# A hymba streaming step on one core: a re-planned instruction order, with 45 weight remainders made by accumulating GpSimd transfers

## The chip, the cores and the metric

The kernel runs on one core of one Trainium2 chip. The metric is the device time of that core in microseconds (us), the median of three executions. One more execution was recorded by the hardware profiler, and all lines of a profile come from it. TensorE (PE in the profile) multiplies matrices; VectorE (DVE), ScalarE (ACT) and GpSimd (POOL) do elementwise work; SyncE (SP) issues the transfers between memory and SBUF. Each engine has its own queue of instructions and takes them in order; semaphores hold an instruction back until what it reads is there.

## The reference

One inference step of an encoder of two layers, on 512 frames of a new stream and 64 frames of a running one, which the kernel treats as one block of 576 columns. A layer is:

```python
proj = x @ w_in                       # 1024 x 2560: q, k, v, conv_a, conv_gate
q, k = rope(q, pos), rope(k, pos)     # 8 sub-heads of 64
a = softmax(q1 k1') - lam * softmax(q2 k2')   # 4 differential heads, masked by chunks
o = rmsnorm(a @ v) * sub_g * (1 - lam_init)
u = conv_a * sigmoid(conv_gate)
c = silu(layer_norm(causal_depthwise_conv(u, hist, conv_w, conv_b)))   # width 31
y = concat(o, c) @ w_out              # 1024 x 1024
x = layer_norm(ALPHA * x + y)
h = square(relu(x @ w_ff1))           # 1024 x 4096
x = layer_norm(ALPHA * x + h @ w_ff2)
```

Outputs are x of both streams, the new keys and values of both layers, and the last 30 columns of u. Everything is float32.

## The kernel before, in words

**Matrix products in three passes.** A float32 operand is split into a rounded part and a remainder. A weight `w` gives `wh` (ScalarE copies `raw` into a type that TensorE reads in one pass, L834) and `wl = raw - wh` (L837, a subtraction on VectorE or GpSimd). The product is `wh*xh + wh*xl + wl*xh`, three matmuls of 128x288 (L706, L707, L708). The columns go in two groups of 288.

**Weights.** The weights lie in DRAM as 92 units of 128x1024 for each layer: 20 for the input projection (conv gates and inputs 0 to 7, and q, k, v of four heads 8 to 19), 8 for the output projection (20 to 27) and 64 for the feed forward. `weights()` brings a unit: a transfer on SP's queue into one of two `raw` tiles, the copy on ScalarE, the subtraction. There are four pairs `wh`/`wl`; a unit makes 48 matmuls (8 blocks of rows, two column groups, three passes). The first two units come in four quarters each, so that TensorE can begin early. For layer 1 the 20 units of the input projection are split ahead of time, during the feed forward of layer 0, and stored to DRAM (`wscr`); they are loaded ready made. In the feed forward most products are Strassen-like, with sums of weight blocks formed on VectorE first (L2030) and split afterwards (L2003, L1831).

**Stages.** Each layer has a mixer (projection, attention heads, convolution, output projection), a layer norm, the feed forward and another layer norm. In the mixer the convolution takes 31 taps for each of four tiles: VectorE multiplies and adds most of them into a PSUM tile `sc` (L1284), ScalarE multiplies the rest into `prod` (L1269), and GpSimd adds those up in `r` (L1272). An attention block goes: scores on TensorE, the maximum on VectorE (L1433), the exponential on ScalarE (L1449), the difference of the two softmaxes on VectorE (L1477, tile `P`), transposes on TensorE (L1486), the product with v (L1515).

**What sets the order.** Nothing in the kernel is issued in the order in which the code stands. Every operation is a node with its engines and the cost on each, what it depends on, what buffers it takes and gives back, and a priority. `Sched.run` plays the whole program through with these costs (`cV`, `cA`, `cG`, `cD`, `cP`, and `delay` from engine to engine) and issues, at each planned moment, the ready node of highest priority; the instructions then stand in each engine's queue in that order. Where a node may run on two engines (a subtraction on VectorE or GpSimd) the plan chooses. VectorE and GpSimd share a port: a node marked `two`, and every node that may run on GpSimd, waits in the plan until the port is free. Planned times only decide the order; on the chip an instruction starts when its semaphores allow. `PHASES` holds eight sets of knobs (priorities, which squares go where, how many taps go to ScalarE and GpSimd) for the mixer, the output projection, the feed forward and its end, in each layer.

Of the kernel before, what the change touches and what calls it, by code (L numbers as in the profile page):

```python
# [135 lines left out]
PRP, PRS = 159.3, -11.0  # L136
# [133 lines left out]
 {'CS': 1,  # L270
  'CSTD': 2,
  'KA': 6,
  'KB': 8,
  'KR': 2,
# [11 lines left out]
  'PE_': 37.6,
  'PK': -502.6,
  'PN': 781.5,
  'PQ': 23.6,
  'PR': 47.2,  # L290
  'PS': 304.1,
  'PT': 1371.8,
# [2083 lines left out]
```

## Time and profile before

| | us |
|---|---|
| median of three executions | 1412.38 (1410.14 to 1413.55) |
| the profiled execution | 1412.93 |
| its span, first to last instruction | 1411.1 |
| TensorE busy | 1318.3 |
| VectorE busy | 1130.2 |
| ScalarE busy | 680.2 |
| GpSimd busy | 268.8 |

Mean granted clock of TensorE 0.969. A busy TensorE in this table is not a TensorE at full speed: matmuls overlap, a matmul counts as busy until its modelled end, and it takes longer under a lower granted clock. Where stages are compared, the number of matmuls begun in a stretch is the better measure. In a row of the stretches ("windows"), each engine has its busy time and in brackets how many instructions; then come the granted clock, the share of the DMA engines, and GB/s. In a list of waits the columns are the total, the number of waits and the longest. In a timeline they are the start, the duration, the engine, line, operation and tiles, and in square brackets the idle time before and what ended it.

### The profile page before, as it was taken

How to read it: one execution, taken by the hardware profiler on the slowest of the kernel's cores; microseconds unless marked ns; L12 is line 12 of the kernel's file. 1: busy time of each engine (PE TensorE's matmuls, PEld its weight loads, DVE VectorE, ACT ScalarE, POOL GpSimd, SP SyncE). 2: the span in 40 equal slices, each digit the busy share in tenths (PEclk: the TensorE clock that was granted, in tenths of full speed). 3: DMA queues.
4: the chain of work that ended last, by engine and by line, in shares of the span. 5: the costliest groups of instructions: out<-in, count | busy, mean ns of one | idle time of the engine just before them, and what ended most of it. 6: DMA issues, size and time to landing. Idle time of an engine off the chain costs nothing.

```text
span 1411.1 us, 24840 instructions
## 1 busy us (share of the span) xinstructions
PE 1318.3 (93%) x9512; PEld 1268.5 (90%) x9512; DVE 1130.2 (80%) x2251; ACT 680.2 (48%) x1388; POOL 268.8 (19%) x246
## 2 busy tenths in 40 slices
PE   6979699979899999999999989899899999999997
PEld 5979588979899999999988988689889999999996
DVE  6799998785888887978739899888768777777756
ACT  4656567254444445444246566642645343434414
POOL 0447510260000000000133684212400000000003
PEclk9999899999999999999999999799899999999998
DMA  6312134134265555555544432222122132313121
GB/s 200 97 61 80 41 105 144 60 98 134 93 196 170 195 162 179 180 179 182 181 151 166 148 127 100 81 86 62 44 83 98 61 120 75 105 61 116 58 68 68
DMA packets 63623, 162.79 MB, mean 115 GB/s; under 512 B 10128, under 2 KB 15888, under 8 KB 63504
## 3 DMA queue, kind: packets, MB, share of 16 engines
q1 hardware_dynamic: 63504, 161.20, 34.5%
q8 instruction: 75, 1.23, 0.4%
q14 instruction: 44, 0.36, 0.1%
HBM read 130.52 MB, written 30.65 MB: 114 GB/s over the span
## 4 chain that ended last, share of the span: by engine, by line
PE 70%; DVE 21%; ACT 4%; issue 2%; DMA 1%; POOL 1%; SPq 0%; ACTq 0%; DVEq 0%; POOLq 0%
PE b L706 21%; PE b L708 21%; PE b L707 21%; DVE sc L1284 7%; PE b L953 1%; DVE nm L1433 1%; DVE wl L837 1%; DVE P L1477 1%; PE b L1515 1%; PE sc L706 1%; PE sc L708 1%; POOL sq L1011 1%; PE sc L707 1%; DVE swp L1314 1%; DMA a<-in_xT_dram 1%
## 5 line engine op out<-in xcount | busy, mean ns | idle before, releaser
L706 PE MATMUL b<-x,wh 128*128 128x288 f32 x1364 | 418.4, 307 | 17.8 <-ACT wh L834 9.0
L708 PE MATMUL b<-x,wl 128*128 128x288 f32 x1364 | 406.9, 298 | 6.5 <-DVE wl L837 5.0
L707 PE MATMUL b<-x,wh 128*128 128x288 f32 x1364 | 406.9, 298 | 1.1 <-POOL x L1101 1.0
L706 PE MATMUL b<-a,wh 128*128 128x288 f32 x1088 | 326.9, 300 | 1.8 <-ACT P L1454 0.9
L707 PE MATMUL b<-a,wh 128*128 128x288 f32 x1088 | 323.1, 297 | 0.0
L708 PE MATMUL b<-a,wl 128*128 128x288 f32 x1088 | 322.4, 296 | 0.0
L706 PEld LDWEIGHTS b<-x,wh 128*128 128x128 f32 x1364 | 260.5, 191 | 27.5 <-ACT wh L834 10.3
L708 PEld LDWEIGHTS b<-x,wl 128*128 128x128 f32 x1364 | 260.1, 191 | 8.5 <-DVE wl L837 6.7
L707 PEld LDWEIGHTS b<-x,wh 128*128 128x128 f32 x1364 | 260.6, 191 | 3.0 <-POOL x L1101 1.8
L706 PEld LDWEIGHTS b<-a,wh 128*128 128x128 f32 x1088 | 206.6, 190 | 3.3 <-ACT P L1454 1.1
L707 PEld LDWEIGHTS b<-a,wh 128*128 128x128 f32 x1088 | 207.0, 190 | 0.5
L708 PEld LDWEIGHTS b<-a,wl 128*128 128x128 f32 x1088 | 206.6, 190 | 0.0
L1011 POOL TENSOR_TENSOR sq<-sq,sq 128x288 f32<-128x288 f32 x41 | 35.2, 883 | 765.5 <-ACT sq L1005 764.9
L834 ACT CAST wh<-raw 128x1024 fp32r<-128x1024 f32 (+1 forms) x118 | 118.7, 1006 | 125.0 <-PE b L707 89.7
L837 DVE TENSOR_TENSOR wl<-raw,wh 128x1024 fp32r<-128x1024 f32 (+1 forms) x113 | 135.4, 1201 | 28.8 <-ACT wh L834 28.4
L2220 DVE TENSOR_TENSOR r<-r,b 128x288 f32<-128x288 f32 x192 | 86.4, 451 | 76.3 <-PE b L708 76.2
L1272 POOL TENSOR_TENSOR r<-r,prod 128x606 f32<-128x606 f32 x75 | 115.9, 1545 | 116.7 <-ACT prod L1269 98.8
L1284 DVE SCALAR_TENSOR_TENSOR sc<-ub,par,sc 128x606 f32<-128x606 f32 x157 | 133.5, 851 | 3.7
L2003 ACT CAST wh<-ckv 128x512 fp32r<-128x512 f32 x104 | 64.0, 620 | 97.8 <-PE b L707 75.1
L1831 DVE TENSOR_TENSOR wl<-ckv,wh 128x512 fp32r<-128x512 f32 x104 | 71.1, 685 | 3.0 <-ACT wh L2003 2.9
L1269 ACT ACTIVATE prod<-ub,par 128x606 f32<-128x606 f32 x75 | 59.3, 802 | 23.2 <-POOL r L1272 22.9
L2003 ACT CAST wh<-ah 128x512 fp32r<-128x512 f32 x52 | 32.2, 620 | 53.3 <-PE b L707 52.2
(321 smaller groups left out, 2286.3 us busy)
## 6 DMA issues: line engine op xcount, KB each, us to landing
raw<-in_wu_dram SPq DMA_DIRECT2D x110, 512.0 KB, 3.7
wscr<-cs SPq DMA_DIRECT2D x80, 256.0 KB, 2.5
ckv<-in_wu_dram SPq DMA_DIRECT2D x26, 512.0 KB, 3.7
ah<-in_wu_dram SPq DMA_DIRECT2D x26, 512.0 KB, 4.4
cs<-in_wu_dram SPq DMA_DIRECT2D x40, 256.0 KB, 2.8
wh<-wscr SPq DMA_DIRECT2D x20, 512.0 KB, 3.3
wl<-wscr SPq DMA_DIRECT2D x20, 512.0 KB, 4.3
ckv<-in_ck_dram SPq DMA_DIRECT2D x8, 512.0 KB, 5.0
```

The lines of the kernel that those rows point to most:

```text
L706: TE.matmul(o, wh, xh, start=start, stop=False)
L707: TE.matmul(o, wh, xl, start=False, stop=False)
L708: TE.matmul(o, wl, xh, start=False, stop=stop)
L834: S.copy(wt["hi"][:, c], wt["raw"][:, c])
L837: e.tensor_tensor(wt["lo"][:, c], wt["raw"][:, c], wt["hi"][:, c].bitcast(F32), op=ALU.subtract)
L1011: e.tensor_tensor(q[a]["t"], q[a]["t"], q[b]["t"], op=ALU.add)
L1269: S.activation(st[j], ub[t][:, j:j + UC], AF.Copy, scale=w)
L1272: GP.tensor_tensor(cc[t], cc[t], st[j], op=ALU.add)
L1284: V.scalar_tensor_tensor(st["a0"], win(j), w, st["a0"], op0=ALU.mult, op1=ALU.add)
L1831: e.tensor_tensor(o, a, b, op=ALU.subtract)
L2003: S.copy(tl["wh"][box["i"]][:, off:off + n], src())
L2220: V.tensor_tensor(rr, rr, bk(), op=ALU.add)
```

## The change

The plan is made with other costs and knobs, and some weight remainders are made by transfers.

1. **45 units by accumulating transfers.** A new knob `DM` says which share of the units of a phase goes this way: 0.67 in the mixer and the output projection of layer 0, 0 in its feed forward, and 1 for the output projection, 0.5 for the feed forward and 1 for its last four units in layer 1. Such a unit is loaded into `raw` as before; ScalarE writes `wl = -raw` (L875 of the changed kernel), GpSimd's queue issues a transfer that reads the same unit from DRAM again and adds it into `wl` (L878), and ScalarE copies `raw` to `wh` (L881). No subtraction is left on VectorE or GpSimd for that unit, and `raw` is given back after the copy to `wh`. So `wl` becomes the difference between the weight and its rounded value. 16 of the 45 are in layer 0 (10 in the input projection, 6 in the output projection), 29 in layer 1 (8 in the output projection, 21 in the feed forward).
2. **The plan's model.** A transfer that only waits for the transfer before it on the queue no longer waits in the plan for that one's landing (`late`). Costs of ScalarE reading a PSUM bank, with one and with two per-partition operands, are told apart; delays between engines are a little smaller; what TensorE waits for gets 0.1 more. In the rule of the port only who is marked changes: the first step of the reciprocal root is marked, and the accumulating transfer is exempt.
3. **The knobs** of all eight phases.

The core of the diff:

```diff
-def cA(n, ptr=False):
-    return (0.19 if ptr else 0.09) + 0.00084 * n
+def cA(n, ptr=0, bank=False):
+    return (0.09 + 0.095 * ptr if not bank else 0.05) + 0.00084 * n
...
-PRP, PRS = 159.3, -11.0
+PD = 0.1
+DM, GD, GDL = 0.0, 0.88, 6.5
+PRP, PRS = 889.2, -10.4
...
-PHASES = [{'CS': 0,
+PHASES = [{'CH': 4,
+  'CS': 0,
   'CSTD': 2,
-  'KA': 2,
+  'DM': 0.67,
+  'KA': 4,
...
     def delay(a, b):
         if a == b:
-            return 0.0 if a in "PDN" else 0.12
+            return {"A": 0.08, "V": 0.03, "G": 0.05}.get(a, 0.0)
         if "N" in (a, b):
             return 0.0
-        return 0.25 if "P" in (a, b) else 0.15
+        return 0.2 if "P" in (a, b) else 0.13
...
+                            late = 0.0 if e == "D" and "D" in s.eng else n.lat
                             for o in s.eng:
-                                s.ready = max(s.ready, t + c + n.lat + min(self.delay(e, o) for o in s.eng))
+                                s.ready = max(s.ready, t + c + late + min(self.delay(e, o) for o in s.eng) + (PD if "P" in s.eng and e in "VAG" else 0.0))
...
+        chain["dm"] += 0.0 if start else DM
+        by_dma = not start and chain["dm"] >= 0.999
+        chain["dm"] -= by_dma
...
+            if by_dma:
+                def neg(e):
+                    slots()
+                    S.activation(wt["lo"], wt["raw"], AF.Copy, scale=-1.0)
+                def acc(e):
+                    GP.dma_start(wt["lo"], wu[l, i], accum_op=ALU.add)
+                def hi(e):
+                    S.copy(wt["hi"], wt["raw"])
+                wt["hin"] = m = op({"A": cA(D)}, neg, (chain["ld"], chain["hi"]), acq=("w",), pri=pri)
+                los.append(op({"G": GD}, acc, (m,), lat=GDL, pri=pri + 1000, two=False))
+                chain["hi"] = h = op({"A": cA(D)}, hi, (m,), rel=end, pri=pri)
+                his.append(h)
+                return
...
-        m = op({"V": 0.27}, start, (dep,), rel=rel, pri=pri)
+        m = op({"V": 0.27}, start, (dep,), rel=rel, pri=pri, two=True)
```

What the change makes of the instructions in all: TensorE's work is the same but for three small matmuls; VectorE's subtractions of 128x1024 for weights go from 105 to 65 and GpSimd's from 5 to none; ScalarE has 45 instructions more, the negations. Three places in the order follow; in them a line number is that of the kernel the rows come from, and the number behind a name tells buffers apart.

**The start, on SP's queue.** `a` are the tiles of x as they come in (eight tiles for each of the two column groups), `raw_81` and `raw_82` the two weight tiles; 128x256 is a quarter of a unit. Before, from the last tile of x on:

```order
L1149 DMA a_209<-in_xT_dram 128x288
L828 DMA raw_81<-in_wu_dram 128x256
L1181 DMA cs_259<-in_cst_dram 128x1152
L699 DMA par_161<-in_par_dram 128x169
L828 DMA raw_82<-in_wu_dram 128x256
L1382 DMA ckv_112<-in_ck_dram 128x1024
L745 DMA sgm_100<-in_par_dram 128x256
L699 DMA ident<-in_cst_dram 128x128
L828 DMA raw_82<-in_wu_dram 128x256
L699 DMA par_165<-in_par_dram 128x169
L745 DMA sgm_101<-in_par_dram 128x256
L828 DMA raw_82<-in_wu_dram 128x256 x2
```

Now, from the fourth quarter of the first unit on:

```order
L861 DMA raw_81<-in_wu_dram 128x256
L861 DMA raw_82<-in_wu_dram 128x256 x3
L1202 DMA a_230<-in_xT_dram 128x288
L861 DMA raw_82<-in_wu_dram 128x256
L1202 DMA a_240<-in_xT_dram 128x288
L1202 DMA a_187<-in_xT_dram 128x288
L861 DMA raw_81<-in_wu_dram 128x1024
L1202 DMA a_190<-in_xT_dram 128x288
L1202 DMA a_193<-in_xT_dram 128x288
L861 DMA raw_82<-in_wu_dram 128x1024
L1202 DMA a_195<-in_xT_dram 128x288
L1202 DMA a_201<-in_xT_dram 128x288
```

The second unit's quarters, the third and the fourth unit moved ahead of most of the second column group of x, and ahead of the tables (`cs`), the parameters and the cache (`ckv`), which come behind x now.

**The convolution of layer 0, on VectorE's queue.** The rows are in the second tile's taps (`ub_795`/`ub_801` is its input, `sc_119` the sum); `P` is the softmax difference of an attention block. Before:

```order
L1284 SCALAR_TENSOR_TENSOR sc_119<-ub_795,par_161,sc_119 128x2x303
L837 TENSOR_TENSOR wl_88<-raw_82,wh_84 128x1024
L1284 SCALAR_TENSOR_TENSOR sc_119<-ub_795,par_161,sc_119 128x2x303
L1477 SCALAR_TENSOR_TENSOR P_914<-P_914,rc_564 64x576
L1284 SCALAR_TENSOR_TENSOR sc_119<-ub_795,par_161,sc_119 128x2x303
L837 TENSOR_TENSOR wl_89<-raw_81,wh_85 128x1024
L1284 SCALAR_TENSOR_TENSOR sc_119<-ub_795,par_161,sc_119 128x2x303
L1322 TENSOR_TENSOR r_94<-r_94,swp_972 128x576
L1284 SCALAR_TENSOR_TENSOR sc_119<-ub_795,par_161,sc_119 128x2x303
L837 TENSOR_TENSOR wl_90<-raw_82,wh_86 128x1024
```

Now, around the same block of the same head:

```order
L1337 SCALAR_TENSOR_TENSOR sc_119<-ub_801,par_161,sc_119 128x2x303 x2
L1530 SCALAR_TENSOR_TENSOR P_921<-P_921,rc_599 64x576
L1337 SCALAR_TENSOR_TENSOR sc_119<-ub_801,par_161,sc_119 128x2x303 x5
L894 TENSOR_TENSOR wl_89<-raw_81,wh_85 128x1024
L1337 SCALAR_TENSOR_TENSOR sc_119<-ub_801,par_161,sc_119 128x2x303
```

Two of the three subtractions left this stretch; the `P` row stands 10 rows earlier in the queue than it did.

**The same stage on GpSimd's queue**, where `r` collects the taps that ScalarE multiplied. Before:

```order
L1272 TENSOR_TENSOR r_91<-r_91,prod_730 128x606
L1239 MEMSET ub_795 128x30
L837 TENSOR_TENSOR wl_87<-raw_81,wh_83 128x1024
L1272 TENSOR_TENSOR r_93<-r_93,prod_871 128x606
L1272 TENSOR_TENSOR r_93<-r_93,prod_886 128x606
```

Now:

```order
L878 DMA wl_88<-in_wu_dram 128x1024
L878 DMA wl_89<-in_wu_dram 128x1024
L1292 MEMSET ub_544 128x30
L1325 TENSOR_TENSOR r_92<-r_92,prod_624 128x606
L878 DMA wl_87<-in_wu_dram 128x1024
L1325 TENSOR_TENSOR r_92<-r_92,prod_633 128x606
L1325 TENSOR_TENSOR r_92<-r_92,prod_653 128x606
```

The subtraction is gone and transfers stand between the additions; each waits there for ScalarE's negation of its unit.

More of the change, by code (lines that the diff above doesn't have):

```diff
@@ L277 @@
   'LD3': 0.18,
-  'LDO': 0,
+  'LDO': 227.3,
   'LDS': 200,
   'LP': 0.67,
-  'LPE': 0.58,
-  'LPT': 0.28,
-  'PA': 1099.3,
+  'LPE': 0.87,
+  'LPT': -0.51,
+  'PA': 523.9,
   'PC': -297.1,
   'PCN': 956.0,
[L286 to L292, printed above, removed]
-  'PW': 491.4,
+  'PE_': 6.7,
+  'PK': -340.0,
+  'PN': 770.8,
+  'PQ': -19.8,
+  'PR': 114.6,
+  'PS': 52.6,
+  'PT': 1584.5,
+  'PV': 322.6,
+  'PW': -395.4,
+  'PX': 306.9,
   'QL0': '0 6 7',
@@ L302 @@
   'SHP': 0,
-  'VP': -0.07,
-  'VS': 1.76,
-  'WP': 0.31,
-  'WP2': -1.1,
-  'WP3': -1.93},
+  'VP': -0.56,
+  'VS': 1.08,
+  'WP': 0.14,
+  'WP2': -1.0,
+  'WP3': -2.02},
  {'CH': 2,
   'CSTD': 2,
+  'DM': 0,
+  'KA': 1,
+  'KB': 4,
+  'KR': 2,
+  'LA': 0.36,
+  'LD1': 1.27,
+  'LD2': 2.31,
+  'LD3': 1.29,
+  'LDO': -40.7,
+  'LDS': 800,
+  'LP': -1.01,
+  'LPE': 0.85,
+  'LPT': -0.43,
+  'NPT': '9,10,12,12',
+  'PA': 632.1,
+  'PC': -524.7,
+  'PCN': 602.4,
+  'PE_': 461.1,
+  'PK': -255.4,
+  'PN': -270.8,
@@ new lines @@
+  'PR': 0.0,
+  'PS': -6.5,
+  'PT': 755.3,
+  'PV': 636.9,
+  'PW': 87.5,
+  'PX': -121.8,
+  'QL0': '0 2 4 6',
+  'QL1': '0 2 4 5 6 7',
+  'QLF': '0 2 4 6 7',
+  'RG': 0,
+  'RP': [0, 3],
+  'RS': 1,
+  'S2F': [5, 7],
+  'S2H': [0, 3, 6, 7],
+  'SHP': 0,
+  'SQ': 'k0 q0 g0 a0 v0 q1 g1 a1 g2 a2 k1 g3 v1 a3 q2 k2 v2 q3 k3 v3',
+  'VP': 0.64,
+  'VS': 1.22,
+  'WP': -0.27,
+  'WP2': -0.69,
+  'WP3': -2.07},
+ {'CS': 1,
+  'CSTD': 2,
+  'DM': 1,
+  'KA': 2,
+  'KB': 7,
+  'KR': 1,
+  'LA': 1,
+  'LD1': 2.07,
+  'LD2': 0.86,
+  'LD3': 1.49,
+  'LDO': -165.8,
+  'LP': 0.9,
+  'LPE': 1.52,
+  'LPT': 0.22,
+  'PA': -314.7,
+  'PC': 346.5,
+  'PCN': 413.1,
+  'PE_': -162.8,
+  'PK': -82.2,
+  'PN': 44.4,
+  'PQ': -8.3,
+  'PR': 218.7,
+  'PS': -201.7,
+  'PT': 1198.7,
+  'PV': 418.8,
+  'PW': 651.6,
+  'QL0': '0 2 4 6',
+  'QL1': '0 6',
+  'QLF': '0 4 6 7',
+  'RG': 1,
+  'RP': [1, 3, 4, 7],
+  'RS': 1,
+  'S2F': [3, 6, 7],
+  'S2H': [4, 7],
+  'VP': -0.28,
+  'VS': -0.19,
+  'WP': 1.15,
+  'WP2': -0.09,
+  'WP3': 1.18},
@@ new lines @@
+ {'CH': 4,
+  'CS': 0,
+  'CSTD': 2,
+  'DM': 0.5,
+  'KA': 4,
+  'KB': 3,
+  'KR': 6,
+  'LA': 0,
+  'LD1': 1.8,
+  'LD2': 1.36,
+  'LD3': 0.75,
+  'LDO': 1124.1,
+  'LP': 1.55,
+  'LPE': 0.09,
+  'LPT': -0.31,
+  'PA': -537.3,
+  'PC': 252.9,
+  'PCN': 826.0,
+  'PE_': 317.9,
+  'PK': -148.1,
+  'PN': 12.5,
+  'PQ': -26.3,
+  'PR': -255.5,
+  'PS': -541.0,
+  'PT': 1328.5,
+  'PV': -307.5,
+  'PW': 222.2,
+  'PX': -295.5,
+  'QL0': '0 4 6 7',
+  'QL1': '0 6',
+  'QLF': '0 2 4 6 7',
+  'RG': 0,
+  'RP': [1, 3, 4, 5],
+  'RS': 1,
+  'S2F': [1, 3, 7],
+  'S2H': [4, 7],
+  'VP': -0.0,
+  'VS': 1.91,
+  'WP': -1.53,
+  'WP2': -1.19,
+  'WP3': 0.12},
@@ L371 @@
+  'LD1': 0.71,
+  'LD2': 1.18,
+  'LD3': 1.09,
+  'LDO': 367.6,
+  'LDS': 1000,
+  'LP': 2.49,
+  'LPE': 1.42,
+  'LPT': 0.13,
+  'PA': 612.8,
+  'PC': 341.3,
+  'PCN': 869.8,
+  'PE_': 261.4,
+  'PK': -256.1,
+  'PN': -96.8,
+  'PQ': -24.5,
+  'PR': -282.1,
+  'PS': -118.4,
+  'PT': 872.7,
+  'PV': 747.8,
+  'PW': -52.3,
+  'PX': -1345.3,
   'QL0': '0 6 7',
@@ L767, in params @@
         return d0, op({"V": 0.4}, f3, (n2, d0))
[L769 removed]
+    chain = {"dm": 0.0, "ld": None, "hi": None, "pe": None}
     pre = {}
```

398 lines of the change are left out of this document (139 added, 259 removed).

## The prediction

> **What bounds the kernel now.** I read the page first, then the stretches between the layer norms, then shorter stretches in the first mixer, then who waits for whom. From the page, the span, the busy times and the chain of work that ended last:
>
> ```profile
> span 1411.1 us, 24840 instructions
> PE 1318.3 (93%) x9512; PEld 1268.5 (90%) x9512; DVE 1130.2 (80%) x2251; ACT 680.2 (48%) x1388; POOL 268.8 (19%) x246
> PE 70%; DVE 21%; ACT 4%; issue 2%; DMA 1%; POOL 1%; SPq 0%; ACTq 0%; DVEq 0%; POOLq 0%
> ```
>
> TensorE is most of the chain, but VectorE has a fifth of it, and the question is where. The stretches, cut where VectorE begins each layer norm (L999): mixer 0, feed forward 0, mixer 1, feed forward 1, end; below them a stretch inside a feed forward.
>
> ```profile
> 0.00:277.10 277.10, 236.52 (x1662) 217.81 (x1663) 237.59 (x450) 157.39 (x338) 90.74 (x75) 0.96 0.32 100
> 277.10:689.70 412.60, 399.49 (x2954) 393.99 (x2953) 329.76 (x662) 186.54 (x353) 28.54 (x31) 0.99 0.48 158
> 689.70:972.90 283.20, 262.11 (x1803) 243.30 (x1802) 233.49 (x452) 151.22 (x343) 113.94 (x97) 0.93 0.36 125
> 972.90:1380.00 407.10, 397.67 (x2948) 393.23 (x2947) 306.65 (x621) 170.27 (x322) 22.86 (x27) 0.99 0.24 78
> 1380.00:1411.10 31.10, 22.45 (x154) 20.13 (x153) 22.70 (x68) 14.78 (x32) 12.71 (x16) 0.78 0.22 77
> ...
> 440.00:480.00 40.00, 40.00 (x303) 40.00 (x302) 34.16 (x71) 17.69 (x32) 0.00 (x0) 1.00 0.58 192
> ```
>
> At full speed TensorE begins 303 matmuls in 40 us, one in 0.132 us. By that measure mixer 0 could have begun 2099 and began 1662: 437 short, 58 us. Mixer 1 is short by 342 (45 us), the feed forwards by 171 and 136 (23 and 18 us), the end by 82 (11 us). The mixers hold two thirds of what is lost. Inside them:
>
> ```profile
> 0.00:35.00 35.00, 22.11 (x122) 18.96 (x123) 21.89 (x50) 16.90 (x36) 0.92 (x13) 1.00 0.66 201
> ...
> 80.00:120.00 40.00, 32.30 (x228) 30.75 (x227) 38.85 (x59) 22.07 (x37) 22.12 (x16) 0.91 0.25 81
> 120.00:160.00 40.00, 29.11 (x217) 27.66 (x215) 38.15 (x55) 22.24 (x44) 34.07 (x23) 0.90 0.13 43
> 160.00:200.00 40.00, 38.24 (x271) 34.38 (x272) 38.13 (x86) 28.06 (x62) 3.77 (x2) 0.93 0.32 102
> 200.00:240.00 40.00, 34.88 (x248) 30.11 (x244) 36.49 (x76) 25.82 (x68) 6.74 (x5) 1.00 0.45 140
> 880.00:920.00 40.00, 32.58 (x161) 26.66 (x161) 32.03 (x68) 23.25 (x56) 11.47 (x9) 0.74 0.29 87
> ```
>
> From 80 to 200 us VectorE has 38 to 39 of every 40 us: it is the bound there. From 880 to 920 it is not (32 of 40), and TensorE still loses 142 matmuls (19 us): that is a chain of small dependent steps. What TensorE waits for over the run, and one such wait in time:
>
> ```profile
> PE b L1486 <- DVE P L1477: 24.7, 10, 10.9
> ```
>
> ```profile
> 148.46 9.73 DVE L1284 SCALAR_TENSOR_TENSOR sc<-ub,par,sc 128x606 f32<-128x606 f32 x11
> 158.10 1.59 DVE L1477 SCALAR_TENSOR_TENSOR P<-P,rc 128x128 f32<-128x128 f32 x1
> ...
> 148.56 0.29 PE L708 MATMUL b<-x,wl 128*128 128x288 f32 x1
> 159.75 0.47 PE L1486 MATMUL b<-ident,P 128*128 128x128 f32 x1 [10.89 <-DVE P L1477]
> ```
>
> `P` stood behind eleven convolution taps on VectorE's queue, and TensorE had run out of projection matmuls. A gap costs more than its length, since the clock falls after it; here the matmuls after a 1.56 us wait follow each other at 0.24 us, not 0.13:
>
> ```profile
> 909.71 1.97 PE L1519 MATMUL b<-ah,ckv 128*128 128x64 f32 x8 [1.56 <-ACT ah L703]
> ...
> 914.08 0.44 PE L707 MATMUL b<-a,wh 128*128 128x288 f32 x1
> 914.32 0.44 PE L708 MATMUL b<-a,wl 128*128 128x288 f32 x1
> ```
>
> **The change part by part.** First the prices of a weight unit on each engine, and where the subtractions lie (VectorE, then GpSimd, in mixer 0, mixer 1 and feed forward 1):
>
> ```profile
> L837 DVE TENSOR_TENSOR wl<-raw,wh 128x1024 fp32r<-128x1024 f32 x105 | 132.0, 1260 | 26.3 <-ACT wh L834 25.9
> L834 ACT CAST wh<-raw 128x1024 fp32r<-128x1024 f32 x110 | 115.5, 1050 | 124.0 <-PE b L707 89.7 <-DMA raw<-in_wu_dram 19.2 <-issue 7.2
> L837 POOL TENSOR_TENSOR wl<-raw,wh 128x1024 fp32r<-128x1024 f32 x5 | 13.1, 2614 | 18.7 <-ACT wh L834 18.7
> ...
> 0.00:277.10 277.10, 30.24 (x30) 10.69 (x4) 0.96 0.32 100
> 689.70:972.90 283.20, 9.75 (x7) 2.38 (x1) 0.93 0.36 125
> 972.90:1380.00 407.10, 47.47 (x38) 0.00 (x0) 0.99 0.24 78
> ```
>
> *The start.* TensorE waits for the first units:
>
> ```profile
> PE b L708 <- DVE wl L837: 3.8, 4, 1.3
> PE b L706 <- ACT wh L834: 3.3, 4, 1.4
> ...
> 5.00:10.00 5.00, 3.11 (x11) 2.55 (x11) 3.83 (x10) 3.65 (x10) 0.00 (x0) 1.00 0.93 268
> 15.00:20.00 5.00, 4.37 (x26) 3.62 (x26) 2.73 (x6) 2.21 (x6) 0.00 (x0) 1.00 0.97 316
> ```
>
> That is 7.1 us between 14 and 36 us; all of the first 35 us is 143 matmuls (19 us) short. The transfers run at 0.93 to 0.97 of the engines, so only their order can help. Now four units stand ahead of the tables and the cache, so TensorE has three units to work on while x arrives. A price of it: the third unit needs `raw_81` again, and waits on SP until the first unit's last subtraction; seven tiles of x of the second group are queued behind it. That quarter lands in a few us and costs a copy and a subtraction of a quarter, well under 2 us, while TensorE has the first group of two units. I take -6, bounds 0 and -10 (half of the 19).
>
> *Mixer 0 after the start.* 12 subtractions leave VectorE (22 full ones stood there in the order, 10 are left): 12 x 1.26 = 15.1 us. Four leave GpSimd, 10.7 us. In return VectorE gets a little: two taps and some small adds, about 2 us. Ten of the 16 units are those of the projection, consumed where VectorE has 95%: there its time is the stage's. The other six are consumed after 240 us, where TensorE is full. So 10 x 1.26 = 12.6 less 2: -10, bounds 0 and -17. The stall at 159.75 also gets cover: 84 more rows stand ahead of that transpose on TensorE's queue, 11 us at 0.132. This is the same time, not a second gain, since VectorE must still do its taps.
>
> *Mixer 1.* The projection's units come ready made, so seven subtractions go, 7 x 1.26 = 8.8 us, and by the rows of the order some 6 us of copies and rotations move to ScalarE and GpSimd. VectorE is at 82% there, and the loss at 880 to 920 is a chain through ScalarE too. I count a third of the 15: -5, bounds 0 and -12.
>
> *Feed forward 1.* 21 subtractions (26 us of VectorE) go. TensorE begins 2948 of 3084 there, and what it misses lies at the ends. Nothing: bounds 0 and -3.
>
> *Feed forward 0, the last layer norm.* Other knobs only: 0, within 3 either way.
>
> *What is added.* ScalarE gets 45 negations of the price of its copy, 45 x 1.05 = 47 us: 17 in mixer 0 where it has 157 of 277, 22 in feed forward 1 where it has 170 of 407. Hidden; without that cover a unit would be 1.05 us later. SP's queue is not moved past. GpSimd's queue gets 45 issues. No transfer from that queue is in this trace. Its issue is bounded by a subtraction it replaces (2.6 us) and by an issue on SP (0.38 us, below); in mixer 0 that is 16 issues on an engine with 91 of 277 us busy. Behind a waiting issue stand the additions `r` (L1272), behind them ScalarE's `prod`, of which there are two; a late negation would show there first. How late the remainder comes is bounded by these rows:
>
> ```profile
> 0.74 0.38 SPq L1149 DMA_DIRECT2D a<-in_xT_dram  x1
> ...
> raw<-in_wu_dram SPq DMA_DIRECT2D x110, 512.0 KB, 3.7
> wscr<-cs SPq DMA_DIRECT2D x80, 256.0 KB, 2.5
> q1 hardware_dynamic: 63504, 161.20, 34.5%
> ```
>
> Below, a load of the same bytes: 3.7 us. Above, load, and two half-size trips each way one after another, and a slow issue: 3.7 + 2 x 2.5 + 2.6 = 11.3. I take 7, nearer to the load, since the two sides of one transfer overlap. The cover: four pairs `wh`/`wl`, 48 matmuls or 6.3 us each, so a pair may be filled while the other three are used, up to 19 us. In layer 0 the tightest pair has 78 rows of TensorE (10.3 us) between its old and its new use, less 1.05 for the negation; in feed forward 1 the plan issues the transfer 72 matmuls ahead, 9.5 us. 7 fits: 0. The extra bytes are 45 x 0.52 = 24 MB against 161; even counted twice they take 10% of the engines beside 34.5%.
>
> The Trainium skill ("DMA: Bandwidth & Descriptors", section on the anatomy of a transfer on the GpSimd path) fits such a transfer at 2.0 us plus bytes over 436 GB/s, which is 3.2 us here. By it the cover would be larger and the sum the same; it says nothing of accumulating, and no run here shows one yet.
>
> The sum: -6 - 10 - 5 = -21. The profiled execution took 1412.9 (span 1411.1 and 1.8 around it), 0.5 over the median; so 1392 for its like, **1391 us** for the median.
>
> **The rivals.**
>
> *A, off the path.* VectorE's time is saved, but the mixers are paced by chains, or GpSimd's issues take the port from VectorE. That the port costs is in the trace: a subtraction that began while GpSimd multiplied took 2.41 us, not 1.26.
>
> ```profile
> 902.75 1.42 POOL L1318 TENSOR_TENSOR r<-r,cs 128x576 f32<-128x576 f32 x1
> 902.84 2.41 DVE L837 TENSOR_TENSOR wl<-raw,wh 128x1024 fp32r<-128x1024 f32 x1
> ```
>
> If each of 16 issues did that, 16 x 1.15 = 18 us would come back in mixer 0, more than the 15 saved, and 9 for 9 in mixer 1. The start stays, less some loss: 1403 to 1415.
>
> The Trainium skill ("SBUF — State Buffer", "Who interferes with whom") says that an op with two SBUF inputs takes only the pair's read side, and infers that writing descriptors needs the write side. By that rule the issues would not hold up subtractions, and rival A keeps only its chains.
>
> *B, slower: the remainder lands late.* One mechanism, at the third matmul of a block (`wl`): TensorE waits for a transfer that is longer than its cover. In feed forward 1 fifteen units have 9.5 us; a landing L us after the issue costs 15 x (L - 9.5) there, and the 21 us are used up at L = 11. At 12.5, 45 us more: 1436. For it: the bound above reaches 11.3, and accumulating reads its target first. Against: 7 us from the nearer rows, and few transfers beside it.
>
> *C, more.* The start gives 10, mixer 0 gives 17, mixer 1 gives 12: 1373.
>
> *D, the plan is not followed.* Better costs move the real order little. That is A's time.
>
> **How the numbers follow.** Forecast 0.56, A with D 0.20, B 0.15, C 0.09. The forecast's own range, with its terms' middles off by half, is 1380 to 1402. 0.3% (4.2 us) is about what a measurement of this kernel can tell from no change. A lies half inside it (0.10), 0.08 faster, 0.02 slower. So faster 0.56 + 0.09 + 0.08 = 0.73, same 0.10, slower 0.17. The range leaves out most of B and the best of C: 1368 to 1416.
>
> **What would show it.** Right: VectorE below 1085 us; the first 35 us with 150 matmuls or more; the 10.9 us wait at L1486 gone; the first layer norm begun near 261 us; no wait of TensorE at the `wl` matmul for an accumulating transfer. Wrong: waits at that matmul in feed forward 1 (B); VectorE's taps or subtractions stretched beside GpSimd's issues, with the layer norm near 275 (A); a mixer 1 as long as before, which takes 5 away.

## The result and the profile after

The changed kernel takes 1374.7 us (median of four, 1370.4 to 1377.9), the kernel before, on the same chip, 1412.5 (1410.1 to 1413.6). The ratio is 0.9733, 95% interval 0.9702 to 0.9763: 37.8 us less, where 21 were forecast. The profiled execution took 1375.7. From its page, the span, the busy times and the chain that ended last:

```profile
span 1373.9 us, 24858 instructions
PE 1308.0 (95%) x9518; PEld 1264.1 (92%) x9518; DVE 1078.1 (78%) x2206; ACT 705.1 (51%) x1413; POOL 302.3 (22%) x292
PE 72%; DVE 18%; issue 3%; DMA 2%; ACT 2%; POOL 2%; SPq 0%; ACTq 0%; DVEq 0%; POOLq 0%
```

By this count TensorE has six small matmuls more than before (9518 for 9512), not three.

The stretches of the changed kernel, cut as before where VectorE begins each layer norm (now L1052), and below them the first 35 us:

```profile
0.00:264.00 264.00, 240.47 (x1662) 223.67 (x1663) 223.63 (x432) 168.85 (x356) 95.21 (x88) 0.95 0.51 137
264.00:675.40 411.40, 398.91 (x2954) 395.41 (x2953) 330.54 (x667) 182.84 (x342) 26.89 (x30) 0.98 0.48 159
675.40:938.10 262.70, 250.59 (x1790) 234.13 (x1790) 216.94 (x437) 154.30 (x349) 127.50 (x112) 0.97 0.49 150
938.10:1343.00 404.90, 396.40 (x2966) 391.72 (x2965) 284.29 (x604) 183.79 (x333) 40.64 (x47) 1.00 0.40 106
1343.00:1373.90 30.90, 21.65 (x155) 19.17 (x153) 22.71 (x68) 15.30 (x33) 12.10 (x15) 0.86 0.23 77
...
0.00:35.00 35.00, 28.43 (x175) 25.94 (x176) 18.74 (x44) 19.87 (x42) 3.17 (x14) 1.00 0.70 221
```

Mixer 0 is 13.1 us shorter, feed forward 0 1.2, mixer 1 20.5, feed forward 1 2.2, the end 0.2. So nearly all of it lies in the two mixers, as forecast, but mixer 1, counted at 5, gave most. Of its 20.5 us, 1.7 are a shift of the cut: 13 matmuls fewer are begun there (1790 for 1803, at 0.132 us each), and feed forward 1 has 18 more. In both mixers VectorE's busy time fell by about what the stage lost: 237.6 to 223.6 in mixer 0 and 233.5 to 216.9 in mixer 1. In feed forward 1 it fell by 22.4 (306.6 to 284.3), and the stage by 2.2.

What TensorE waits for in the changed kernel (line numbers have moved: L1539 and L1541 are the transposes of `P`, of which only L1486 waited for VectorE before; L736 is the matmul with `wl`):

```profile
PE b L736 <- DVE wl L894: 4.8, 1, 4.8
PE b L1541 <- DVE P L1530: 4.4, 1, 4.4
PE b L1539 <- DVE P L1530: 4.3, 3, 1.9
...
PE b L736 <- DMA wl<-in_wu_dram: 1.9, 2, 1.2
```

The transposes waited 24.7 us for `P` before; now it is 8.7, at L1539 and L1541 together. For the accumulating transfers TensorE waits twice, 1.9 us in all. The one place of the 10.9 us wait, in time:

```profile
156.89 2.62 DVE L1337 SCALAR_TENSOR_TENSOR sc<-ub,par,sc 128x606 f32<-128x606 f32 x3
159.42 0.34 DVE L1530 SCALAR_TENSOR_TENSOR P<-P,rc 128x128 f32<-128x128 f32 x1
...
159.82 0.33 PE L1539 MATMUL b<-ident,P 128*128 128x128 f32 x1 [1.94 <-DVE P L1530]
```

Fewer taps stand ahead of `P` at a time, and TensorE has projection matmuls until 1.94 us before it. The new operations themselves, from the groups, the queues and the DMA issues of the page, and last the answer on the issuing line's landings:

```profile
L878 POOL DMA_DIRECT2D wl<-in_wu_dram x45 | 39.2, 871 | 446.8 <-ACT wl L875 387.6
L875 ACT ACTIVATE wl<-raw 128x1024 fp32r<-128x1024 f32 x45 | 47.7, 1060 | 44.2 <-PE b L736 25.5
...
q1 hardware_dynamic: 63504, 161.20, 34.9%
q0 software_dynamic: 6480, 23.60, 10.4%
...
raw<-in_wu_dram SPq DMA_DIRECT2D x110, 512.0 KB, 4.6
wl<-in_wu_dram POOLq DMA_DIRECT2D x45, 512.0 KB, 7.2
...
DMA to landing us min/median/max: 5.2/7.2/9.9
```

An issue takes GpSimd 0.87 us, a negation 1.06 us of ScalarE, and the transfer lands 7.2 us after its issue (estimated: 7). The Trainium skill ("DMA: Bandwidth & Descriptors", the anatomy of a transfer on the GpSimd path) gives 2.0 us plus bytes over 436 GB/s, 3.2 us for these bytes; the trace does not agree for an accumulating transfer, whose shortest is 5.2. Weight loads on SP's queue now land in 4.6 us, before in 3.7.

### The profile page after: what moved, and what is told of

Its sections match the earlier page's. It is cut to its first block, busy times and chain, and to the rows that moved or that the text cites. A ratio compares the mean times of both kernels' runs of the same rounds, so it can differ in the third digit from the quotient of the medians.

```text
span 1373.9 us, 24858 instructions
## 1 busy us (share of the span) xinstructions
PE 1308.0 (95%) x9518; PEld 1264.1 (92%) x9518; DVE 1078.1 (78%) x2206; ACT 705.1 (51%) x1413; POOL 302.3 (22%) x292
## 3 DMA queue, kind: packets, MB, share of 16 engines
q1 hardware_dynamic: 63504, 161.20, 34.9%
q0 software_dynamic: 6480, 23.60, 10.4%
## 4 chain that ended last, share of the span: by engine, by line
PE 72%; DVE 18%; issue 3%; DMA 2%; ACT 2%; POOL 2%; SPq 0%; ACTq 0%; DVEq 0%; POOLq 0%
PE b L734 21%; PE b L735 21%; PE b L736 21%; DVE sc L1337 8%; DMA raw<-in_wu_dram 2%; PE sc L734 1%; PE b L1006 1%; POOL sq L1064 1%; PE sc L736 1%; PE b L1568 1%; PE sc L735 1%; DVE nm L1486 1%; DVE P L1530 1%; DMA wl<-in_wu_dram 1%; PE b L1611 1%
## 5 line engine op out<-in xcount | busy, mean ns | idle before, releaser
L736 PE MATMUL b<-x,wl 128*128 128x288 f32 x1356 | 406.1, 299 | 7.0 <-DVE wl L894 4.8
L736 PE MATMUL b<-a,wl 128*128 128x288 f32 x1088 | 321.0, 295 | 0.0
L736 PEld LDWEIGHTS b<-x,wl 128*128 128x128 f32 x1356 | 260.2, 192 | 8.2 <-DVE wl L894 5.3
L736 PEld LDWEIGHTS b<-a,wl 128*128 128x128 f32 x1088 | 205.1, 188 | 0.0
L878 POOL DMA_DIRECT2D wl<-in_wu_dram x45 | 39.2, 871 | 446.8 <-ACT wl L875 387.6
L891 ACT CAST wh<-raw 128x1024 fp32r<-128x1024 f32 (+1 forms) x73 | 71.4, 979 | 71.2 <-PE b L735 52.3
L894 DVE TENSOR_TENSOR wl<-raw,wh 128x1024 fp32r<-128x1024 f32 (+1 forms) x73 | 84.5, 1161 | 22.3 <-ACT wh L891 21.7
L875 ACT ACTIVATE wl<-raw 128x1024 fp32r<-128x1024 f32 x45 | 47.7, 1060 | 44.2 <-PE b L736 25.5
```

Of the source, the lines that this page charges most:

```text
L736: TE.matmul(o, wl, xh, start=False, stop=stop)
L875: S.activation(wt["lo"], wt["raw"], AF.Copy, scale=-1.0)
L891: S.copy(wt["hi"][:, c], wt["raw"][:, c])
L894: e.tensor_tensor(wt["lo"][:, c], wt["raw"][:, c], wt["hi"][:, c].bitcast(F32), op=ALU.subtract)
```

## The experiments

All times are medians of four to ten executions (kernels 2, 4 and 10 have ten, kernel 6 eight). The ratio is to the kernel before on the same chip, whose median was 1411.3 to 1413.2 there. The stages are those of one execution each, the profiled one, in us. The executions of one kernel lie 3 to 13 us apart; stages with the same instructions in the same order agree better (the mixers of kernel 11 and of the change within 0.5 us).

| kernel | median | ratio to before, 95% | mixer 0 | ff 0 | mixer 1 | ff 1 | end |
|---|---|---|---|---|---|---|---|
| before | 1412.5 | | 277.1 | 412.6 | 283.2 | 407.1 | 31.1 |
| the change | 1374.7 | 0.970 to 0.976 | 264.0 | 411.4 | 262.7 | 404.9 | 30.9 |
| 1 its order, subtractions | 1395.6 | 0.985 to 0.990 | 274.4 | 411.5 | 269.5 | 406.2 | 29.9 |
| 2 old order, transfers | 1414.0 | 0.999 to 1.002 | 281.9 | 416.9 | 277.8 | 405.4 | 30.2 |
| 3 no transfers, planned anew | 1403.1 | 0.990 to 0.995 | 282.9 | 410.7 | 271.8 | 405.1 | 30.4 |
| 4 new model, old knobs, no transfers | 1408.5 | 0.995 to 0.998 | 288.5 | 409.2 | 265.1 | 410.8 | 31.2 |
| 5 the same with transfers | 1398.0 | 0.987 to 0.994 | 276.8 | 410.2 | 272.6 | 409.6 | 31.4 |
| 6 the change with the old `late` | 1402.6 | 0.993 to 0.996 | 278.7 | 412.4 | 274.3 | 405.8 | 30.3 |
| 7 the change, old knobs for mixer 1 | 1393.2 | 0.985 to 0.989 | 264.9 | 411.6 | 277.6 | 407.2 | 30.8 |
| 8 the change, old knobs for mixer 0 | 1391.2 | 0.983 to 0.988 | 273.8 | 414.4 | 264.0 | 405.9 | 31.3 |
| 9 every transfer twice | 1553.1 | 1.095 to 1.104 | 325.1 | 410.8 | 288.4 | 486.8 | 30.3 |
| 10 before with the new `late` | 1408.4 | 0.996 to 0.999 | 279.5 | 412.1 | 276.6 | 409.4 | 30.3 |
| 11 the change, feed forward 1 by subtractions | 1373.0 | 0.971 to 0.973 | 263.5 | 411.6 | 262.7 | 404.7 | 30.3 |
| 12 all of mixer 0 by transfers | 1397.8 | 0.986 to 0.991 | 281.2 | 414.1 | 267.4 | 406.4 | 30.3 |

### Order and transfers apart (1 and 2)

Kernel 1 is the changed kernel with its order word for word; no negation, no transfer, and a subtraction on VectorE right behind the copy to `wh`:

```diff
                 def neg(e):
                     slots()
-                    S.activation(wt["lo"], wt["raw"], AF.Copy, scale=-1.0)
                 def acc(e):
-                    GP.dma_start(wt["lo"], wu[l, i], accum_op=ALU.add)
+                    pass
                 def hi(e):
                     S.copy(wt["hi"], wt["raw"])
+                    V.tensor_tensor(wt["lo"], wt["raw"], wt["hi"].bitcast(F32), op=ALU.subtract)
```

> The new order on every engine, word for word, but the 45 remainders are made by a subtraction on VectorE again, put into its queue right behind the place where ScalarE writes wh; no negation and no accumulating transfer. Theory 1 (the gain is the work taken off VectorE): 45 x 1.23 = 55 us come back on VectorE, 10 to 12 of the units in its bound stretch of mixer 0 and 8 in mixer 1; mixer 0 longer by 10 to 15, mixer 1 by 5 to 15, 1390 to 1405. Theory 2 (the gain is the new order, the transfers only ride along): 1375 to 1382, mixers as in the changed kernel within 3 us.

Kernel 2 is the kernel before with its order word for word, in which the same 45 units are negated and transferred where they were copied and subtracted:

```diff
+                if by_dma:
+                    S.activation(wt["lo"][:, c], wt["raw"][:, c], AF.Copy, scale=-1.0)
                 S.copy(wt["hi"][:, c], wt["raw"][:, c])
...
             def lo(e):
+                if by_dma:
+                    GP.dma_start(wt["lo"], wu[l, i], accum_op=ALU.add)
+                    return
                 e.tensor_tensor(wt["lo"][:, c], wt["raw"][:, c], wt["hi"][:, c].bitcast(F32), op=ALU.subtract)
```

> The old order, word for word, with the same 45 units made by negation and accumulating transfer in place of the subtraction; the plan knows nothing of it. Theory 1: VectorE is freed where it was the bound, mixer 0 shorter by 8 to 12 and mixer 1 by 3 to 8, 1392 to 1402, unless the 7.2 us of landing come too late for an order that put the units' use close behind their making; then TensorE waits for the transfer and the time is above 1410. Theory 2: 1405 to 1415.

The order alone gives about 17 us (1395.6), the transfers alone nothing in the whole (1414.0), both 38. So the transfers are worth some 21 us in the order that was planned for them. Kernel 1's time is the first theory's, but work taken off VectorE explains only these 21 of the 38; kernel 2's time is the second theory's. The first mixer of both, and kernel 2's wait at the transpose of `P` over the whole run:

```profile
0.00:274.40 274.40, 239.67 (x1662) 221.94 (x1663) 241.05 (x447) 153.73 (x340) 86.06 (x72) 0.95 0.32 101
```

```profile
0.00:281.90 281.90, 241.16 (x1662) 221.20 (x1663) 223.68 (x437) 171.23 (x354) 91.42 (x88) 0.95 0.49 128
...
PE b L1498 <- DVE P L1489: 21.3, 10, 9.2
```

In kernel 2 VectorE is relieved as much as in the changed kernel (223.7 us in mixer 0). Mixer 1 is 5.4 us shorter than before and feed forward 1 1.7, but mixer 0 is 4.8 and feed forward 0 4.3 us longer. TensorE waits nowhere for an accumulating transfer, so a late remainder is not the reason. In mixer 0 `P` still stands behind its row of taps, and TensorE's wait for it fell only from 21.1 to 17.7 us. And nearly all that mixer 0 lost, 4.3 us, was lost at one place, which starts at ScalarE:

```profile
109.69 0.62 ACT L706 CAST ckh<-ckv 128x512 fp32r<-128x512 f32 x1 [3.53 <-DMA ckv<-in_ck_dram]
...
125.19 0.55 PE L1369 MATMUL sc<-ident,r 128*128 128x128 f32 x3 [2.59 <-ACT r L706]
```

The load of the cache `ckv` took 7.6 us there from issue to landing, beside an accumulating transfer (100.98 to 108.23 us) and the load of a unit; in the kernel before it took 4.5, and ScalarE waited 1.01 us for it, not 3.53. ScalarE's later copies come that much later, and the negations between them add to it. The 60 matmuls around TensorE's wait take 12.2 us for 7.8 before. So the traffic of the transfers and the negations are not free in an order that has no place for them. Why feed forward 0, in which no unit was changed, is longer stays open.

From kernel 1 to the change, with the order held, mixer 0 loses 10.4 us and mixer 1 6.8: these are the transfers' share. Half of the 10.4 is one wait of TensorE, in kernel 1 and in the change:

```profile
PE sc L734 <- DVE r L1344: 8.6, 1, 8.6
```

```profile
PE sc L734 <- DVE r L1344: 3.2, 1, 3.2
```

A matmul of the attention scores waits for the PSUM tile that the convolution holds until VectorE has added its sum up (L1344). In kernel 1, where VectorE is busy 241.1 of mixer 0's 274.4 us, two subtractions more stand ahead of that sum from 118 us on.

### What the transfers must be planned with (3, 4, 5)

Kernel 3 is the changed kernel with `DM` at 0 in all phases, planned anew:

```diff
-  'DM': 0.67,
+  'DM': 0,
```

> The changed kernel with the share of accumulating transfers set to 0 in all phases and planned anew; the new model and the new knobs stay. Theory 1: VectorE has the 40 subtractions back and the plan can only place them well, 1388 to 1400. Theory 2: 1375 to 1383.

Kernel 4 has the new model with the eight sets of knobs of before, and no transfers; kernel 5 is the same with the new `DM` (the last line, which kernel 4 does not have):

```diff
-PRP, PRS = 889.2, -10.4
+PRP, PRS = 159.3, -11.0
-PHASES = [{'CH': 4,
+PHASES = [{'CS': 0,
...
     g.update(PHASES[i])
+    g["DM"] = (0.67, 0.67, 0.0, 0.0, 0.0, 1.0, 0.5, 1.0)[i]
```

> The new model of the plan (transfers that only follow a transfer, costs, delays) with all the old knobs and no accumulating transfers. If the model alone orders the work better: 1385 to 1400, the start and mixer 1 shorter. If the knobs carry it: 1405 to 1418, since they were chosen for the other model.

> The new model and the 45 accumulating transfers, with all the old knobs (and the old priorities of the units split ahead). Against the new model with old knobs without transfers (1408.5; mixer 0 288.5, mixer 1 265.1) it shows what the transfers are worth where the plan knows of them: 10 in mixer 0 and 7 in mixer 1 if as in the new order, 1388 to 1396. If they only pay with their own knobs: 1400 to 1412. What is left to 1374.7 is the knobs.

Without transfers the new plan takes 1403.1: 28 more than with them, above the first theory's range, and 7.5 more than kernel 1, whose order had been planned for transfers it does not make. Kernel 4's time is in the range for "the knobs carry it", although its mixer 1 became shorter, as the other theory had it. Kernel 5 takes 1398.0, between its two ranges; against kernel 4 its mixer 0 is 11.7 us shorter (10 was expected), but its mixer 1 is 7.5 longer (7 shorter was expected). The knobs are the remaining 23.

The mixers do not move together: kernel 4, with the old knobs and all its subtractions, has mixer 1 at 265.1, nearly the changed kernel's, and mixer 0 at 288.5, longer than before. A new plan moves a mixer by some 10 us either way, for reasons that these runs do not tell. No run has knobs that were chosen for the new model without transfers, so what the transfers are worth beside the best such order is not shown.

### The `late` rule (6 and 10)

Kernel 6 gives the changed kernel the old rule, kernel 10 the kernel before the new one:

```diff
-                            late = 0.0 if e == "D" and "D" in s.eng else n.lat
+                            late = n.lat
```

> The changed kernel, planned with the old rule that a transfer waits for the landing of the one before it (all else new). In the plan a unit of mixer 1 then comes as two transfers of 1.43 + 2.2 us each, 7.3 us, more than the 6.3 us that TensorE takes for it; with the new rule 2.9 us. Theory L (mixer 1 was ordered for loads that are not slow on the chip): mixer 1 goes from 263 back to 275 to 285, the rest within 5 us; 1385 to 1400. Theory K (knobs and costs carry mixer 1): mixer 1 within 5 us of 263, 1372 to 1382.

> The kernel before with that one rule changed and nothing else: same knobs, costs and delays, no accumulating transfers. Theory L: mixer 1 shorter by 10 to 18 us (283 to 265 to 273); mixer 0 may move either way, since its knobs were chosen with the other rule; 1396 to 1408. Theory K: 1408 to 1418, mixer 1 within 5 us of 283.

The first 35 us of kernel 6, and then of kernel 10 with its whole mixer 0:

```profile
0.00:35.00 35.00, 23.33 (x115) 20.16 (x116) 22.18 (x50) 17.24 (x36) 0.86 (x12) 0.95 0.63 199
```

```profile
0.00:35.00 35.00, 28.99 (x181) 26.79 (x182) 19.51 (x44) 19.02 (x41) 0.92 (x13) 1.00 0.70 223
...
0.00:279.50 279.50, 245.39 (x1662) 226.37 (x1663) 234.63 (x448) 160.28 (x342) 81.83 (x72) 0.92 0.32 99
```

The early start comes from this one rule: all kernels with it begin 172 to 181 matmuls in 35 us, all with the old one (before, 2, 6) 115 to 122. In the plan a load no longer waits for the landing of the one ahead of it, so the loads of the first units go out in front of the tables. But by itself the early start is not kept. Kernel 10 had begun 983 matmuls after 160 us against 886 before, but 1379 against 1400 after 240 us, and its mixer 0 is 2.4 us longer. In between it has a stall of 8.8 us for `P`, like the one of 10.9 before, and a granted clock of 0.82. VectorE has all its subtractions there still (234.6 us); that this is why was not tested by itself.

Taking the rule from the changed kernel costs 28 us, adding it to the kernel before gains 3 to 4. In mixer 1 it is worth 6.6 alone and 11.6 in the changed kernel. Kernel 6 lies just above theory L's range and its mixer 1 just below the 275 named there, but mixer 0 grew by 14.7 us where the theory had 5 at most. Kernel 10 is at the lower end of theory K's range, its mixer 1 between the two.

### The knobs of each mixer (7 and 8)

The changed kernel with the old knobs, `DM` kept, in mixer 1 and its output projection (7), or in mixer 0 and its output projection (8); of kernel 7 the first of them, one key to a line:

```diff
   'KA': 1,
-  'KB': 4,
-  'KR': 2,
+  'KB': 8,
+  'KR': 3,
...
```

> The new kernel with the old knobs for the mixer and the output projection of layer 1 (DM kept), replanned. With the new model and the old knobs everywhere, mixer 1 took 265.1 us without transfers and 272.6 with them, against 262.7 in the new kernel and 283.2 before. If the new knobs carry mixer 1's gain, mixer 1 is 270 to 275 and the whole 1383 to 1388. If the new model (the loads no longer spaced) carries it and the rest is chance of the plan, mixer 1 is within 4 of 262.7 and the whole within 5 of 1375. Mixer 0 and the feed forward of layer 0 should stay as in the new kernel (264 and 411).

> The new kernel with the old knobs for the mixer and the output projection of layer 0 (DM 0.67 kept), replanned. With old knobs everywhere mixer 0 took 276.8 us with transfers and 288.5 without. Theory that the knobs and the transfers are both needed in mixer 0: mixer 0 is 274 to 280, the whole 1386 to 1392. Rival, that the knobs of the other phases made the difference between 276.8 and 264.0: mixer 0 is 262 to 268 and the whole within 5 of 1375.

Mixer 1 is 277.6 and the whole 1393.2, more than either theory said; mixer 0 is 273.8 and the whole 1391.2, the first theory's to 0.2 us. With the transfers in the plan, each mixer loses most of its gain with the old knobs; kernel 4 had a short mixer 1 with old knobs, but without transfers. In kernel 7 VectorE has 222.6 us in mixer 1 (233.5 before, 216.9 in the changed kernel), and 15 of the 20 us were lost all the same. The stage, and TensorE's waits for `P` within it:

```profile
676.50:954.10 277.60, 256.26 (x1790) 240.24 (x1789) 222.58 (x440) 155.83 (x346) 129.09 (x111) 0.94 0.46 142
...
PE b L1207 <- DVE P L1196: 4.9, 3, 4.1
PE b L1205 <- DVE P L1196: 4.4, 3, 2.5
```

The waits for `P` (here L1205 and L1207) are 9.3 us; they were 3.6 before, and in the changed kernel's mixer 1 the list of waits has none of them.

### A remainder that comes late (9)

The rival on the slower side was tested by making each remainder late: `wl` starts as -2 `raw`, and the transfer is issued twice, the second waiting for the first.

```diff
-                    S.activation(wt["lo"], wt["raw"], AF.Copy, scale=-1.0)
+                    S.activation(wt["lo"], wt["raw"], AF.Copy, scale=-2.0)
...
                     GP.dma_start(wt["lo"], wu[l, i], accum_op=ALU.add)
+                    GP.dma_start(wt["lo"], wu[l, i], accum_op=ALU.add)
```

> The changed kernel's plan, but each remainder is made by two accumulating transfers one after the other onto -2 w, so it comes after some 15 us (2 x 7.2 + 0.9) instead of 8, and is twice as large (this leaves a small wrong part in the products, of no effect on time). It tests the cover that was counted: 9.5 us ahead in feed forward 1, 10 to 19 in the mixers. If that is the cover, 15 units of feed forward 1 wait some 5 us each, 75 us, and the mixers some more: 1440 to 1470, with the waits at the third matmul of a block. If instructions run further ahead than the plan has them, less: 1376 to 1400.

It takes 1553.1, 178 us more and above the range expected (the profiled execution, whose stages are given, 1543.1). In feed forward 1, the waits of GpSimd's second issue (L879) and of TensorE, and in mixer 0 GpSimd's queue in time:

```profile
POOL wl L879 <- DMA wl<-in_wu_dram: 115.2, 17, 9.4
...
PE b L736 <- DMA wl<-in_wu_dram: 51.6, 17, 6.2
```

```profile
51.31 0.86 POOL L879 DMA_DIRECT2D wl<-in_wu_dram  x1 [8.28 <-DMA wl<-in_wu_dram]
...
61.58 0.86 POOL L879 DMA_DIRECT2D wl<-in_wu_dram  x1 [4.55 <-DMA wl<-in_wu_dram]
62.14 8.03 POOL L1326 TENSOR_TENSOR r<-r,prod 128x606 f32<-128x606 f32 x5
```

Feed forward 1 is 82 us longer: TensorE waits 17 times there, 3.0 us on the average, and its clock falls from 1.00 to 0.93 of full speed. So the mechanism of rival B exists, and its place is the one named. But mixer 0 grew by 61 us and mixer 1 by 26, and in mixer 0 TensorE's waits for a transfer are only 5.2 us. There the second issue holds up GpSimd's queue, 104.9 us in all, with the additions `r` behind it, and TensorE waits 13.9 us for the convolution's sum (L1345) that needs them, and 10.8 for `P`. The expectation had left that out.

### Fewer and more transfers (11 and 12)

Kernel 11 keeps the changed kernel's order and puts back subtractions for the 21 units of feed forward 1 (as in kernel 1); kernel 12 raises `DM` from 0.67 to 1 for the phases of mixer 0, planned anew:

```diff
+                sub = l == 1 and i >= 28
...
-  'DM': 0.67,
+  'DM': 1.0,
```

> The new kernel's order word for word, with the 21 accumulating transfers of feed forward 1 put back to subtractions on VectorE behind the copy; the 24 transfers of the two mixers and output projections stay. Feed forward 1 took 406.2 us with all its subtractions in this order, and 404.9 with the transfers. Theory that a transfer is worth something only where VectorE is what the stage waits for: feed forward 1 is 405 to 407 and the whole within 3 of 1375. Rival, that the feed forward's transfers gave part of the gain in the whole (by memory traffic, or by VectorE at the end of the stage): 1380 or more.

> The new kernel with every unit of layer 0's input and output projection (beyond the first four or so) by a transfer, DM 1.0 for 0.67, replanned: six or seven subtractions less on VectorE in mixer 0, 8 us of it. Theory that VectorE's work sets mixer 0: it goes from 264 to 256 to 260 and the whole to 1367 to 1372. Rival, that a new plan scatters a stage by some 10 us whatever is saved, as mixer 1 did with the same knobs (265, 273 and 278): mixer 0 is 264 to 275 and the whole 1375 to 1387.

Kernel 11 takes 1373.0, feed forward 1 404.7, as the first theory had it: its 21 transfers are worth nothing. VectorE carries 22.9 us more there, beside a full TensorE. The 24 in the mixers and output projections do all the work.

Kernel 12 makes eight transfers more in mixer 0 and takes 1397.8, beyond what either theory allowed: mixer 0 is 281.2. VectorE's subtractions fall by 10.8 us there, yet VectorE is busy 5.4 us more than in the changed kernel. GpSimd's queue has eight issues more (6.9 us), some rotations and sums stand on VectorE now that stood on GpSimd, and some of VectorE's instructions became very long. The worst, from the timeline, with what GpSimd did meanwhile:

```profile
93.91 0.88 POOL L878 DMA_DIRECT2D wl<-in_wu_dram  x1
...
94.25 5.28 DVE L1596 TENSOR_TENSOR osq<-ob 128x576 f32<-128x576 f32 x1
94.52 1.76 POOL L1325 TENSOR_TENSOR r<-r,prod 128x606 f32<-128x606 f32 x1
95.92 0.42 POOL L1292 MEMSET ub<- 128x30 f32 x1
96.00 1.69 POOL L1371 TENSOR_TENSOR r<-r,cs 128x576 f32<-128x576 f32 x1
97.36 1.54 POOL L1445 TENSOR_TENSOR ckl<-ckv,ckh 128x512 fp32r<-128x512 f32 x1
...
99.58 1.60 PE L1006 MATMUL b<-ones_c,osq 128*96 128x1 f32 x9 [5.28 <-DVE osq L1596]
```

The same operation took 0.76 us in kernel 8 (the group's row there):

```profile
L1262 DVE TENSOR_TENSOR osq<-ob 128x576 f32<-128x576 f32 x1 | 0.8, 758 | 0.9 <-ACT ob L397 0.9
```

The operation ended 0.63 us after the last of GpSimd's four instructions, which is about its own length: VectorE was held until they were through, and TensorE stood for 5.28 us. That is part of the 17 us which mixer 0 lost to kernel 12's plan; how the rest divides is open. The changed kernel has such a case too, behind the 4.4 us at L1541 above: at 87.92 us the row of `P` took 3.82 us for 0.82, and ended 0.63 us after the third of three GpSimd instructions. Both began while GpSimd was issuing a transfer.

## Why the prediction was right, and where not

**The sum.** 1391 was forecast and 1374.7 measured, inside the range. Direction and place were right. The number lies at rival C's 1373, but not for C's reasons: C gave the start and mixer 0 27 us and mixer 1 12; measured are 13.1 and 20.5. The time lies outside the forecast's own range of 1380 to 1402; it is in the whole range because that was drawn as far as rival C, and that is luck.

**The start, -6.** The count of matmuls is right: 53 more after 35 us, 7.0 us at 0.132. Kernels 6 and 10 show that it comes from the order of the loads. That it may be added to mixer 0's term is wrong. Kernel 10 has it and keeps none of it in mixer 0. Kernels 3, 4 and 5 have it too, with mixer 0 at 282.9, 288.5 and 276.8 us, 277.1 before. In kernel 1 the whole new order, with the start in it, gives mixer 0 2.7 us. It is a gain only in an order that can use it.

**Mixer 0 after the start, -10.** Forecast with the start -16, measured -13.1. By kernel 1 the transfers give 10.4 of it, what the term said. But "its time is the stage's" is not enough: with the order held, 17.4 us of VectorE's time (241.1 to 223.6) were worth 10.4, and kernel 2 took as much off VectorE as the change and won nothing in this stage. The condition that the sum did not name is the order. I had called the cover of the stalled transpose the same time and not a second gain. No run moves the row of `P` alone. That it moved is not enough: in kernels 5, 8 and 12 TensorE waits only 2.7, 2.1 and 4.6 us for `P` in mixer 0 (21.1 before, 8.7 in the change), and mixer 0 takes 276.8, 273.8 and 281.2.

**Mixer 1, -5: the step that failed.** "I count a third of the 15" priced only what leaves VectorE, and put the new order at nothing beyond that. For the transfers the size was nearly right: 6.8 us by kernel 1, 5.4 by kernel 2. The order gave 13.7 more, by kernel 1 (1.7 of it the shift of the cut), in which VectorE's busy time fell by only 5.6 us (233.5 to 227.9). I had argued that the loss from 880 to 920 us is a chain through ScalarE, which less work on VectorE would not shorten. Mixer 1 in pieces of 40 us from its start, the first two, the fifth and the sixth, before and after:

```profile
689.70:729.70 40.00, 38.31 (x270) 37.21 (x269) 20.94 (x64) 21.69 (x52) 19.77 (x26) 0.91 0.47 165
729.70:769.70 40.00, 36.50 (x245) 33.37 (x244) 34.27 (x55) 21.59 (x51) 11.99 (x9) 0.91 0.49 174
...
849.70:889.70 40.00, 35.94 (x269) 32.55 (x268) 37.66 (x75) 25.19 (x60) 11.92 (x8) 1.00 0.26 94
889.70:929.70 40.00, 34.13 (x170) 29.60 (x171) 31.64 (x58) 18.79 (x38) 11.70 (x9) 0.70 0.35 107
```

```profile
675.40:715.40 40.00, 39.07 (x287) 38.05 (x287) 23.83 (x67) 19.88 (x49) 19.98 (x26) 0.96 0.45 166
715.40:755.40 40.00, 38.97 (x286) 36.37 (x285) 33.02 (x60) 22.78 (x55) 14.86 (x11) 1.00 0.58 200
...
835.40:875.40 40.00, 34.65 (x223) 30.09 (x222) 36.06 (x80) 29.12 (x72) 16.32 (x13) 0.89 0.47 118
875.40:915.40 40.00, 38.88 (x267) 34.31 (x268) 30.12 (x75) 27.46 (x66) 7.01 (x9) 0.94 0.52 139
```

In the sixth TensorE begins 267 matmuls for 170, at a clock of 0.94 for 0.70, with VectorE nearly as busy as before; with the fifth, 490 for 439, which is 6.7 us. The first two give 58 more (7.7 us), where VectorE is not full in either kernel. So the chain was no floor: other work stands now where it left TensorE idle, and the granted clock came back with it. Taking the `late` rule or this mixer's knobs from the changed kernel costs 11.6 and 14.9 us there (6 and 7); but kernel 4 has the rule, the old knobs and all subtractions, and its mixer 1 is at 265.1. So which part of model and knobs gives the 13.7, and how much of it is a lucky plan, stays open.

**Feed forward 1, 0.** Right: -2.2, of which kernels 1 and 11 give the transfers 1.3 at most.

**Feed forward 0 and the end, 0 within 3.** Right: -1.2 and -0.2.

**What is added.** The landing (7, measured 7.2) and the cover were right, though not to the last: TensorE waits twice at the `wl` matmul for a transfer, 1.9 us. Negations and traffic are hidden in this order; in kernel 2's they are part of what mixer 0 lost. The issue, bounded by 0.38 and 2.6 us, takes 0.87.

**Rival A** fell in the main. VectorE's time was on the path, and an issue alone does not hold VectorE up: in the changed kernel 84 VectorE instructions overlap an issue and no other GpSimd instruction, and none takes over 10% more than the shortest of its kind. From the timeline of the changed kernel's feed forward 1, where GpSimd has nothing but the issue:

```profile
1309.67 0.86 POOL L878 DMA_DIRECT2D wl<-in_wu_dram  x1 [8.58 <-ACT wl L875]
1309.73 0.46 DVE L1884 TENSOR_TENSOR a<-sgm,a 128x288 fp32r<-128x288 f32 x1 [3.60 <-ACT a L1891]
```

An addition with both inputs in SBUF takes 0.46 us beside an issue, and the sums and squares of that size take 0.45 to 0.46 beside the other issues of that stage. This is as the Trainium skill has it ("SBUF — State Buffer", "Who interferes with whom"), there by inference. Whether an issue has a part where other GpSimd work follows at once, as in the 3.82 us of the `P` row above, is open. **Rival B** has the right mechanism: kernel 9 shows it, and the cover of the changed kernel is enough. **Rival D** fell: the plan moved the real order, and kernel 1 gives that order 17 us.

**The signs named:** VectorE below 1085 (1078.1), 150 matmuls in 35 us (175), the 10.9 us wait gone (1.94) came true, but kernel 2 has the first (1084.5) and kernel 10 the second (181), and kernel 2 gained nothing and kernel 10 3 to 4 us; the first layer norm is at 264.0 for 261; no wait for a transfer at the `wl` matmul was nearly true.

## What to carry to other kernels

Relief of an engine shows in the time only where that engine ends the stage's waits and the order lets the others use it: the same 45 transfers were worth nothing in the whole in the old order, where mixer 1 won 5 us and mixer 0 lost as much, and 21 us in one planned for them, and 21 of them next to nothing in either. Price the order by itself: here it was 17 of the 38 us. An early start can be lost again behind it, so such terms are not to be added. A plan with one rule or knob changed moves a stage by 10 us for reasons that the edit does not tell; try an edit with the order held word for word first.
